# Two units of the samples' scores above one another in one tile, and zero rows below operands of few rows

## Chip, cores and metric

The kernel runs on one core of a Trainium2 chip. The metric is the time of one execution on the device in microseconds (us); the median of several executions is compared. TensorE multiplies matrices: its left operand has up to 128 rows (the partitions, over which it sums) and up to 128 columns, and it is loaded before the right operand streams through. VectorE, ScalarE and GpSimd do element work, and SyncE issues transfers; GpSimd also issues the gathers.

## What is computed

One inference step of a small decoder with two layers: a gated short convolution, then an attention over a shared latent (256 numbers a position) and a rotary key (32 numbers). One prompt of 1024 positions goes through it, and 8 samples with 4 new positions each, which attend to 2048 cached positions in 16 pages of 128. The part of a sample, cut to what the change touches:

```python
past_c  = cache_ckv[page_table].reshape(8, 2048, 256)      # gathered pages
past_kr = cache_krope[page_table].reshape(8, 2048, 32)
keys = concatenate([concatenate([past_c, c_new], 1), concatenate([past_kr, kr_new], 1)], -1)
q    = concatenate([einsum('blhd,chd->blhc', q_nope, w_uk), q_rope], -1)   # 16 heads
s    = einsum('bqhd,bkd->bhqk', q, keys) * SCALE            # 4 positions x 16 heads = 64 rows
p    = softmax(where(k_pos <= q_pos, s, neg))
o    = einsum('bhqk,bkc->bqhc', p, latent values)           # then w_uv, gate, w_out_mla
```

## The kernel before

The program runs in stages: the convolution layer (to about 500 us), the projections to latents and queries (to about 800), the prompt's attention (816 to 1085), a passage (to 1130), the samples' attention (to 1311), and the rest of the output projection (to 1370). A scheduler sets the order of instructions on every engine when the kernel is built, from the order of the code, the buffers of each pool, and its own simulation of time.

The samples' loop runs over 32 units: 8 samples of 4 units, each of 4 pages, 512 positions. All products are made of a high and a low part of their operands (`hi_of` on ScalarE, `lo_of` on VectorE or GpSimd), so three matmuls stand for one product. Step s of the loop

- issues a gather of latents, `cn`, five units ahead, on GpSimd's queue (`gather`, through `fetch`), and of rotary keys, `kn`, once a sample;
- turns the next unit's `cn` by eight 128x128 transposes on TensorE into `pc`, from which `ch` and `cl` are made (`take`);
- computes scores (`scores`): `ps` has 64 rows of products with the high part of the query and, below them, 64 with the low part; ScalarE copies the low half to `t`, and VectorE adds the halves into `st` and keeps the maximum in `tops`. After a sample's fourth unit `softmax` forms the maximum, the exponentials with their sums, and the reciprocal;
- turns the weights of the unit five steps back (`turn`): four transposes of `st`, 64 rows each, and for the fourth unit one of `own`, the weights of the 4 new positions; the result `pt` has a high and a low part;
- splits `cn` into `nh` and `nl` (`halve`), and weighs the unit six steps back (`weigh`): four pairs of products `po` with `nh` and `nl`, and behind the fourth unit two with `cvl` and `cvh`, the new positions' latents of all samples (32 rows);
- closes a sample seven steps back (`close`): sums the halves of `po` into `ot`, divides, and turns it by two transposes into `olt`.

Between these stand matmuls of the output projection (`left`, tile `pf`; 8 blocks of 24) as fill; they need `wmh` and `wml`, made from transfers `wor` on SyncE's queue. The last stage's products are `pr`. Buffers limit the run ahead: 9 of `cn`, 3 of `nh` and `nl`, 2 of `pt`, 2 of `st` (one a sample).

For the prompt, `divisors` writes the reciprocals of the softmax's sums, split in high and low parts, into four rows by SyncE's transfers, and `times` multiplies them on TensorE by `both`, a matrix of ones and zeros with four rows on partitions 64 to 67, so that 128 columns get their divisors. Seven pairs of heads do this with `rows` (the last four rows of `kr`) in the prompt's stage; the eighth uses `rr` in the passage.

Names in rows: `pc<-ident,cn` is a transpose by the identity matrix; `pp<-ident,st`, `pp<-ident,own` and `pp<-ident,ot` are the turns of weights, of own weights and of a finished sample; `pb<-rr,both` and `pm<-kr,both` are the divisors. In the profile's words PE is TensorE, PEld its loads of the left operand, DVE is VectorE, ACT ScalarE, POOL GpSimd, SP SyncE. Line L69 is the helper `mm`, L74 `hi_of`, L79 `lo_of`; the other lines are in the listing.

Of the kernel before, what the change touches and what calls it, by code (L numbers as in the profile page):

```python
# [21 lines left out]
P = 128  # L22
# [32 lines left out]
def decoder_step(ctx: ExitStack, tc: tile.TileContext, i, o):  # L55
# [611 lines left out]
    tops = new.tile([DN, NB, 5], F32, name="tops")  # L667
    both = new.tile([2 * DR + 4, P], F32R, name="both")[2 * DR:]
# [8 lines left out]
    krh, krl, rows = kr[:DR], kr[DR:2 * DR], kr[2 * DR:, :SEQ]  # L677
# [58 lines left out]
    dve.tensor_copy(both, both_)  # L736
# [173 lines left out]
    def new_scores():  # L910
# [7 lines left out]
        dve.tensor_reduce(tops[:, :, 4], fresh, AX.X, ALU.max)  # L918
# [163 lines left out]
    def divisors(lc, pl, rr_):  # L1082
# [7 lines left out]
        for x in range(2):  # L1090
            for n, src in enumerate((rh, rl)):
                sp.dma_start(f(rr_[2 * x + n:2 * x + n + 1]).rearrange("a (b c) -> a b c", c=8), f(src[:, x]))
# [214 lines left out]
    with ExitStack() as l8:  # L1307
# [33 lines left out]
        rr_ = sc.tile([2 * DR + 4, SEQ], F32R, tag="olt", name="rr")[2 * DR:]  # L1341
        divisors(pairs[NH // 2 - 1], new, rr_)

        sums = sc.tile([DN, NB, 4], F32, name="sums")
        own = sc.tile([DN, NB * (TS + LS)], F32, name="own")
        cv = sw.tile([TS, KV], F32, tag="ot", name="cv", bufs=1)
        cvh = sc.tile([TS, KV], F32R, name="cvh")
        cvl = sc.tile([TS, KV], F32R, name="cvl")

        sp.dma_start(cv, cnd)  # L1350
        hi_of(cvh, cv)
        lo_of(cvl, cv, cvh)
        pool.memset(own, 0.0)
# [61 lines left out]
        def scores(b, g):  # L1415
# [5 lines left out]
            t = sch.tile([DN, 512], F32, tag="t", name="t", bufs=2)  # L1421
            act.activation(t, ps[DN:], AF.Copy)
            if g == 0:
                state["s", b] = sw.tile([P, 4, 512], F32, tag="st", name="st")
            dve.tensor_tensor_reduce(state["s", b][:DN, g], ps[:DN], t, 1.0, NEG, ALU.add, ALU.max, tops[:, b, g:g + 1])

        def softmax(b):
            st = state["s", b]
            m = sw.tile([DN, 2], F32, tag="m", name="m")
            dve.tensor_reduce(m[:, 0:1], tops[:, b], AX.X, ALU.max)  # L1430
            dve.tensor_scalar(m[:, 1:2], m[:, 0:1], -SCALE, None, ALU.mult)
            mine = own[:, (TS + LS) * b:(TS + LS) * b + LS]
            act.activation(mine, fresh[:, b], AF.Exp, scale=SCALE, bias=m[:, 1:2], accum_out=sums[:, b, 0:1])
            for n in range(2):
                act.activation(st[:DN, 2 * n:2 * n + 2], st[:DN, 2 * n:2 * n + 2], AF.Exp, scale=SCALE, bias=m[:, 1:2], accum_out=sums[:, b, n + 1:n + 2])
# [290 lines left out]
```

## Time and profile before

| what | value |
|---|---|
| median of 3 executions | 1366.18 us (1363.27 to 1369.87) |
| the profiled execution | 1371.72 us, span of its trace 1369.9 us, mean granted clock of TensorE 0.971 |
| busy, share of the span | PE 95%, PEld 85%, DVE 63%, ACT 49%, POOL 44% |
| transfers | 131.87 MB, 96 GB/s in the mean |

All rows come from the one profiled execution. A row of a timeline gives the start, the duration, the engine, the line, the operation, result and operands, the shapes (64*128 is a left operand of 64 rows and 128 columns), and in brackets how long the engine had been idle before and what ended that. The starts of neighbouring matmuls are better to go by than their durations, which are modelled and overlap. A row of a window gives its bounds and length, the busy time of PE, PEld, DVE, ACT and POOL with the number of instructions, the granted clock of TensorE (1.00 is 2.4 GHz, 0.50 is 1.2), the busy share of the DMA engines, and GB/s. In the chain of waits every step is followed back from the last instruction to what released it.

### The profile page before, as it was taken

The page shows a single profiled execution, that of the slowest core. Times are in us where ns is not written, and L with a number is a line of the kernel's source. Part 1 is how long each engine was busy: PE and PEld are TensorE (multiplying, and loading weights), DVE is VectorE, ACT ScalarE, POOL GpSimd, SP SyncE. Part 2 cuts the span into 40 slices and gives each one's busy share as a digit, 9 for nine tenths or more (in the row PEclk, how much of TensorE's full clock was granted, in tenths as well). Part 3 has the DMA queues.
Part 4 walks back from the last instruction along what each step waited for, and adds up shares of the span by engine and source line. Part 5 has one row for each costly group of instructions (what it writes and reads, how often), then busy time and mean ns, then how long its engine had stood idle before and what let it go on. Part 6 is the DMA issues. An engine that isn't in the chain of part 4 may idle for free.

```text
span 1369.9 us, 22910 instructions
## 1 busy us (share of the span) xinstructions
PE 1295.0 (95%) x8142; PEld 1167.1 (85%) x8142; DVE 861.7 (63%) x1749; ACT 672.7 (49%) x1394; POOL 605.4 (44%) x828
## 2 busy tenths in 40 slices
PE   6899999999999999998899999999999878999997
PEld 6799999999978899998899878888888756777675
DVE  5776566666464445156623577877778668676865
ACT  5533333333243333222312377777767668777831
POOL 5465555555311133453320555555546634544421
PEclk8899999999999999999999999999999978999999
DMA  6122122122362232346730120121111276444454
GB/s 187 52 64 62 51 76 79 48 79 63 94 220 92 91 110 68 98 133 178 198 91 1 39 63 25 48 63 41 48 47 26 72 215 168 148 130 128 128 163 163
DMA packets 107022, 131.87 MB, mean 96 GB/s; under 512 B 21007, under 2 KB 80059, under 8 KB 106907
## 3 DMA queue, kind: packets, MB, share of 16 engines
q1 hardware_dynamic: 101659, 111.51, 27.6%
q0 software_dynamic: 5248, 18.88, 4.6%
q8 instruction: 65, 1.06, 0.3%
q14 instruction: 50, 0.41, 0.1%
HBM read 93.95 MB, written 28.78 MB: 90 GB/s over the span
## 4 chain that ended last, share of the span: by engine, by line
PE 72%; DMA 10%; DVE 8%; ACT 3%; issue 3%; POOL 2%; SPq 1%; DVEq 0%; POOLq 0%; ACTq 0%
PE pa L69 11%; PE b L69 10%; PE po L69 8%; PE c L69 7%; PE ps L69 7%; PE a L69 6%; PE pm L69 6%; PE pz L69 5%; PE pr L69 3%; DMA qh<-qdh 3%; PE pf L69 3%; DMA cn<-in_cache_ckv_dram,crow 2%; PE pk L69 2%; PE pt L69 1%; DVE mx L1044 1%
## 5 line engine op out<-in xcount | busy, mean ns | idle before, releaser
L79 DVE TENSOR_TENSOR wl<-raw,wh 128x512 fp32r<-128x512 f32 x86 | 71.3, 831 | 87.6 <-ACT wh L74 84.3
L74 ACT ACTIVATE wh<-raw 128x512 fp32r<-128x512 f32 x88 | 55.1, 630 | 129.7 <-PE pa L69 47.0
L1188 ACT ACTIVATE p<-ps 128x512 f32<-128x512 f32 (+1 forms) x192 | 93.2, 492 | 39.7 <-PE ps L69 32.1
L69 PE MATMUL pz<-ph,v 128*128 128x512 f32 (+3 forms) x384 | 104.5, 358 | 0.0
L74 ACT ACTIVATE ph<-p 128x512 fp32r<-128x512 f32 (+1 forms) x192 | 95.4, 526 | 17.8 <-POOL p L1193 16.8
L79 POOL TENSOR_TENSOR pl<-p,ph 128x512 fp32r<-128x512 f32 (+2 forms) x75 | 82.4, 1108 | 33.8 <-ACT ph L74 23.9
L79 DVE TENSOR_TENSOR pl<-p,ph 128x512 fp32r<-128x512 f32 (+3 forms) x117 | 81.0, 706 | 21.5 <-ACT ph L74 21.2
L79 POOL TENSOR_TENSOR nl<-cn,nh 128x256 fp32r<-128x256 f32 x64 | 59.8, 950 | 76.2 <-ACT nh L74 60.9
L1044 DVE TENSOR_REDUCE mx<-pm 128x1 f32<-128x16 f32 (+6 forms) x210 | 83.7, 423 | 9.9 <-PE pm L69 9.5
L1193 POOL TENSOR_SCALAR_AFFINE_SELECT p<-p 128x127 f32<-128x127 f32 (+1 forms) x128 | 47.4, 374 | 75.0 <-ACT p L1188 66.1
L69 PEld LDWEIGHTS pz<-ph,v 128*128 128x128 f32 x384 | 67.0, 193 | 6.4 <-ACT ph L74 0.3
L69 PE MATMUL ps<-qh,kh 97*128 97x512 f32 (+3 forms) x192 | 68.7, 358 | 1.9 <-DMA qh<-mr 0.9
L69 PE MATMUL pz<-pl,v 128*128 128x512 f32 (+1 forms) x192 | 69.0, 360 | 0.7 <-DVE pl L79 0.3
L69 PE MATMUL ps<-qh,kl 97*128 97x512 f32 (+3 forms) x192 | 66.9, 348 | 0.0
L69 PE MATMUL ps<-ql,kh 97*128 97x512 f32 (+3 forms) x192 | 66.8, 348 | 0.0
L69 PE MATMUL pa<-x1h,wh 128*128 128x352 f32 x288 | 64.3, 330 | 1.1 <-DVE big L861 1.1
L69 PE MATMUL pm<-kh,qh 128*128 128x144 f32 (+6 forms) x210 | 60.2, 340 | 5.4 <-DMA qh<-qdh 4.0
L74 ACT ACTIVATE wh<-s 128x512 fp32r<-128x512 f32 x48 | 30.0, 630 | 68.2 <-POOL s L174 27.2
L69 PE MATMUL pa<-x1h,wl 128*128 128x352 f32 x288 | 63.4, 326 | 0.0
L69 PE MATMUL pa<-x1l,wh 128*128 128x352 f32 x288 | 62.5, 325 | 0.0
L109 POOL TENSOR_SCALAR ta<-ss 128x1 f32<-128x1 f32 (+2 forms) x36 | 8.6, 240 | 118.9 <-ACT xa L624 51.1
L79 DVE TENSOR_TENSOR wl<-s,wh 128x512 fp32r<-128x512 f32 x45 | 44.3, 987 | 20.5 <-ACT wh L74 18.8
(483 smaller groups left out, 4426.6 us busy)
## 6 DMA issues: line engine op xcount, KB each, us to landing
raw<-in_w_in_conv_dram SPq DMA_DIRECT2D x32, 512.0 KB
raw<-in_w_in_mla_dram SPq DMA_DIRECT2D x12, 512.0 KB
qdh<-qxh SPq DMA_DIRECT2D x24, 256.0 KB
qdl<-qxl SPq DMA_DIRECT2D x24, 256.0 KB
qh<-qdh SPq DMA_DIRECT2D x16, 384.0 KB
ql<-qdl SPq DMA_DIRECT2D x16, 384.0 KB
raw<-in_w_out_conv_dram SPq DMA_DIRECT2D x8, 512.0 KB
x1d<-xa SPq DMA_DIRECT2D x8, 512.0 KB
```

The source lines that it names most:

```text
L69: return pe.matmul(out, a, b, start=start, stop=stop, **kw)
L74: return act.activation(out, src, AF.Copy, scale=scale)
L79: (eng or dve).tensor_tensor(out, src, f(hi), ALU.subtract)
L109: pool.tensor_scalar(t[:r], ss[:r], 1.0 / n, EPS, ALU.mult, ALU.add)
L1044: dve.tensor_reduce(mx[:, b, c:c + 1], pm[:, :off], AX.X, ALU.max)
L1188: act.activation(pt[:r, :n], ps[:r, :n], AF.Exp, scale=SCALE)
L1193: marks[h] = marks.get(h, []) + [pool.affine_select(pt[:r, :dn], pt[:r, :dn], [[1, dn]], ALU.is_ge, 0.0, base=META + c0 - t * P, channel_m ...
```

## The change

Two units share one tile of 128 partitions. The scores of an even unit go to partitions 0 to 63 and those of an odd unit to 64 to 127 of an `st` of 512 columns, of which there are five buffers instead of two of four times the width. `tops` and `sums` get 128 rows, and the maximum and the sums are joined over the two halves by small instructions of VectorE. The exponential runs twice over 128x512 instead of twice over 64x1024. `turn` transposes two units at once, by four 128x128 transposes, and `pt` holds both. The own positions get a turn of their own (`turn_own`), 128 columns of a `own` with 128 rows. Operands with few rows get zero rows up to 128 (`own`, `cvh`, `cvl`, `ot`), or 68 (`both`, `rows`, `rr`). The lags of the loop stay as they are. The weights `w_uv` come in four transfers into four tiles of `st`. The diff below leaves out context and the changed slices in the products of `w_uv`.

```diff
@@ -664,8 +664,8 @@
-    tops = new.tile([DN, NB, 5], F32, name="tops")
-    both = new.tile([2 * DR + 4, P], F32R, name="both")[2 * DR:]
+    tops = new.tile([P, NB, 3], F32, name="tops")
+    both = new.tile([2 * DR + 4, P], F32R, name="both")
@@ -674,7 +674,7 @@
-    krh, krl, rows = kr[:DR], kr[DR:2 * DR], kr[2 * DR:, :SEQ]
+    krh, krl, rows = kr[:DR], kr[DR:2 * DR], kr[:, :SEQ]
@@ -733,7 +733,8 @@
-    dve.tensor_copy(both, both_)
+    pool.memset(f(both[:2 * DR]), 0.0)
+    dve.tensor_copy(both[2 * DR:], both_)
@@ -915,7 +916,8 @@
-        dve.tensor_reduce(tops[:, :, 4], fresh, AX.X, ALU.max)
+        pool.memset(tops[DN:, :, 2], NEG)
+        dve.tensor_reduce(tops[:DN, :, 2], fresh, AX.X, ALU.max)
@@ -1089,7 +1091,7 @@
-                sp.dma_start(f(rr_[2 * x + n:2 * x + n + 1]).rearrange("a (b c) -> a b c", c=8), f(src[:, x]))
+                sp.dma_start(f(rr_[2 * DR + 2 * x + n:2 * DR + 2 * x + n + 1]).rearrange("a (b c) -> a b c", c=8), f(src[:, x]))
@@ -1338,19 +1340,23 @@
-        rr_ = sc.tile([2 * DR + 4, SEQ], F32R, tag="olt", name="rr")[2 * DR:]
+        rr_ = sc.tile([2 * DR + 4, SEQ], F32R, tag="olt", name="rr")
+        pool.memset(f(rr_[:2 * DR]), 0.0)
...
-        sums = sc.tile([DN, NB, 4], F32, name="sums")
-        own = sc.tile([DN, NB * (TS + LS)], F32, name="own")
-        cv = sw.tile([TS, KV], F32, tag="ot", name="cv", bufs=1)
-        cvh = sc.tile([TS, KV], F32R, name="cvh")
-        cvl = sc.tile([TS, KV], F32R, name="cvl")
...
-        sp.dma_start(cv, cnd)
-        hi_of(cvh, cv)
-        lo_of(cvl, cv, cvh)
-        pool.memset(own, 0.0)
+        sums = sc.tile([P, NB, 4], F32, name="sums")
...
+        own = sc.tile([P, TS * (NB - 1) + P], F32, name="own")
+        cvh = sc.tile([P, KV], F32R, name="cvh")
+        cvl = sc.tile([P, KV], F32R, name="cvl")
+        ot = sc.tile([P, KV], F32, name="ot")
...
+        for t in (ot, sums, own, f(cvh), f(cvl)):
+            pool.memset(t, 0.0)
+        sp.dma_start(ot[:TS], cnd)
+        hi_of(cvh[:TS], ot[:TS])
+        lo_of(cvl[:TS], ot[:TS], cvh[:TS])
@@ -1418,42 +1424,51 @@
-            t = sch.tile([DN, 512], F32, tag="t", name="t", bufs=2)
-            act.activation(t, ps[DN:], AF.Copy)
-            if g == 0:
-                state["s", b] = sw.tile([P, 4, 512], F32, tag="st", name="st")
-            dve.tensor_tensor_reduce(state["s", b][:DN, g], ps[:DN], t, 1.0, NEG, ALU.add, ALU.max, tops[:, b, g:g + 1])
+            mine, other = (slice(0, DN), slice(DN, P))[::1 - 2 * (g % 2)]
+            t = sch.tile([P, 512], F32, tag="t", name="t", bufs=2)
+            act.activation(t[mine], ps[other], AF.Copy)
+            if g % 2 == 0:
+                state["s", b, g // 2] = sw.tile([P, 512], F32, tag="st", name="st", bufs=5)
+            dve.tensor_tensor_reduce(state["s", b, g // 2][mine], ps[mine], t[mine], 1.0, NEG, ALU.add, ALU.max, tops[mine, b, g // 2:g // 2 + 1])
...
-            st = state["s", b]
-            m = sw.tile([DN, 2], F32, tag="m", name="m")
+            m = sw.tile([P, 3], F32, tag="m", name="m")
...
-            dve.tensor_scalar(m[:, 1:2], m[:, 0:1], -SCALE, None, ALU.mult)
-            mine = own[:, (TS + LS) * b:(TS + LS) * b + LS]
-            act.activation(mine, fresh[:, b], AF.Exp, scale=SCALE, bias=m[:, 1:2], accum_out=sums[:, b, 0:1])
+            dve.tensor_copy(m[:DN, 1:2], m[DN:, 0:1])
+            for rr in (slice(0, DN), slice(DN, P)):
+                dve.tensor_scalar(m[rr, 2:3], m[:DN, 0:1], m[:DN, 1:2], -SCALE, ALU.max, ALU.mult)
...
-                act.activation(st[:DN, 2 * n:2 * n + 2], st[:DN, 2 * n:2 * n + 2], AF.Exp, scale=SCALE, bias=m[:, 1:2], accum_out=sums[:, b, n + 1:n + 2])
-            dve.tensor_reduce(sums[:, b, 3:4], sums[:, b, :3], AX.X, ALU.add)
-            dve.reciprocal(sums[:, b, 3:4], sums[:, b, 3:4])
...
-        def turn(b, g):
...
-            st = state["s", b]
-            if b == NB - 1:
-                pp = pss.tile([P, 512], F32, tag="s", name="pp")[:, :5 * DN].rearrange("p (n c) -> p n c", c=DN)
-            else:
-                pp = psp.tile([P, 5, DN], F32, tag="p", name="pp")
-            for n in range(4):
-                pe.transpose(pp[:, n], st[:DN, g, n * P:(n + 1) * P], ident[:DN, :DN])
-            pt = sw.tile([P, 5, P], F32R, tag="pt", name="pt", bufs=PTB)
-            if g == 3:
-                pe.transpose(pp[:TS, 4], own[:, TS * b:TS * b + TS], ident[:DN, :DN])
-                hi_of(pt[:TS, 4, :DN], pp[:TS, 4])
-            hi_of(pt[:, :4, :DN], pp[:, :4])
-            if g == 3:
-                lo_of(pt[:TS, 4, DN:], pp[:TS, 4], pt[:TS, 4, :DN])
-            lo_of(pt[:, :4, DN:], pp[:, :4], pt[:, :4, :DN])
-            state["q", b, g] = pt
+                st = state["s", b, n]
+                act.activation(st, st, AF.Exp, scale=SCALE, bias=m[:, 2:3], accum_out=sums[:, b, n + 1:n + 2])
+            mine = own[:DN, (TS + LS) * b:(TS + LS) * b + LS]
+            act.activation(mine, fresh[:, b], AF.Exp, scale=SCALE, bias=m[:DN, 2:3], accum_out=sums[:DN, b, 0:1])
...
+        def turn(b, n):
...
+            st = state.pop(("s", b, n))
...
+            pp = (pss.tile([P, 4, 2, DN], F32, tag="s", name="pp") if b == NB - 1 else psp.tile([P, 4, 2, DN], F32, tag="p", name="pp"))
+            for k in range(4):
+                pe.transpose(pp[:, k].rearrange("p e c -> p (e c)"), st[:, k * P:(k + 1) * P], ident)
+            pt = sw.tile([P, 4, 2, P], F32R, tag="pt", name="pt", bufs=PTB)
+            hi_of(pt[:, :, :, :DN], pp)
+            lo_of(pt[:, :, :, DN:], pp, pt[:, :, :, :DN])
+            state["q", b, n] = pt
...
+        def turn_own(b):
...
+            pp = psp.tile([P, 4, 2, DN], F32, tag="p", name="pp")
+            pe.transpose(pp[:, 0].rearrange("p e c -> p (e c)"), own[:, TS * b:TS * b + P], ident)
+            pt = sw.tile([P, P], F32R, tag="po", name="pto", bufs=3)
+            hi_of(pt[:, :DN], pp[:, 0, 0])
+            lo_of(pt[:, DN:], pp[:, 0, 0], pt[:, :DN])
+            state["q", b, "own"] = pt
...
+            s = sums[:, b]
+            dve.tensor_reduce(s[:, 3:4], s[:, :3], AX.X, ALU.add)
+            dve.tensor_copy(s[:DN, 0:1], s[DN:, 3:4])
+            dve.tensor_tensor(s[:DN, 3:4], s[:DN, 3:4], s[:DN, 0:1], ALU.add)
+            dve.reciprocal(s[:DN, 3:4], s[:DN, 3:4])
@@ -1467,7 +1482,7 @@
-            pt = state.pop(("q", b, g))
+            pt = state["q", b, g // 2][:, :, g % 2]
@@ -1477,19 +1492,20 @@
-                mm(po[:DN], pt[:TS, 4, :DN], cvl, False, False)
-                mm(po, pt[:TS, 4], cvh, False, True)
+                pt = state.pop(("q", b, "own"))
+                mm(po[:DN], pt[:, :DN], cvl, False, False)
+                mm(po, pt, cvh, False, True)
...
-            t = sw.tile([DN, KV], F32, tag="ot", name="ot", bufs=1)
+            t = ot[:DN]
...
-            dve.tensor_scalar(t, t, sums[:, b, 3:4], None, ALU.mult)
-            pp = psp.tile([P, 5, DN], F32, tag="p", name="pp")
+            dve.tensor_scalar(t, t, sums[:DN, b, 3:4], None, ALU.mult)
+            pp = psp.tile([P, 4, 2, DN], F32, tag="p", name="pp")
...
-                pe.transpose(pp[:, c], t[:, c * P:(c + 1) * P], ident[:DN, :DN])
-            act.activation(olt[:, :, :, LS * b:LS * b + LS], pp[:, :2].rearrange("p c (h t) -> p c h t", t=LS), AF.Copy)
+                pe.transpose(pp[:, c].rearrange("p e c -> p (e c)"), ot[:, c * P:(c + 1) * P], ident)
+            act.activation(olt[:, :, :, LS * b:LS * b + LS], pp[:, :2, 0].rearrange("p c (h t) -> p c h t", t=LS), AF.Copy)
@@ -1560,7 +1576,13 @@
-            for lag, what in ((LAGT, turn), (LAGH, halve), (LAGW, weigh)):
+            if 0 <= s_ - LAGT < len(units):
+                b, g = units[s_ - LAGT]
+                if g % 2 == 0:
+                    turn(b, g // 2)
+                elif g == 1:
+                    turn_own(b)
+            for lag, what in ((LAGH, halve), (LAGW, weigh)):
```

Order on GpSimd in the passage, before: `kn` and `cn` are gathers, and the fill of `own` stands between them.

```order
L1339 DMA cn<-in_cache_ckv_dram,crow 128x1024
L1339 DMA kn<-in_cache_krope_dram,krow 128x512
L1353 MEMSET own 64x288
L1339 DMA cn<-in_cache_ckv_dram,crow 128x1024 x6
L1339 DMA kn<-in_cache_krope_dram,krow 128x512
```

And after:

```order
L1341 DMA kn<-in_cache_krope_dram,krow 128x512
L1344 MEMSET rr 64x1024
L1356 MEMSET ot 128x256
L1356 MEMSET sums 128x32
L1356 MEMSET own 128x352
L1356 MEMSET cvh 128x256
L1356 MEMSET cvl 128x256
L1341 DMA cn<-in_cache_ckv_dram,crow 128x1024 x6
```

Six fills now stand ahead of the six gathers, where one stood.

Order on ScalarE in the passage, before: `ch` is a turned unit's high part, `wmh` that of the output weights, `kh` that of the rotary keys.

```order
L74 ACTIVATE cvh<-cv 32x256
L1422 ACTIVATE t<-ps 64x512
L74 ACTIVATE kh<-kx 128x512
L74 ACTIVATE ch<-pc 128x512 x3
L74 ACTIVATE wmh_12807<-wor 128x512
L74 ACTIVATE ch<-pc 128x512
L74 ACTIVATE wmh_12808<-wor 128x512
```

And after:

```order
L74 ACTIVATE cvh<-ot 32x256
L74 ACTIVATE wmh_12814<-wor 128x512
L74 ACTIVATE wmh_12815<-wor 128x512
L74 ACTIVATE ch<-pc 128x512 x4
L74 ACTIVATE wmh_12816<-wor 128x512
```

Two conversions of output weights stand ahead of the four `ch` instead of between them.

Order on TensorE around one turn in the middle of the loop, before:

```order
L69 MATMUL pf<-wmh_12814,gl 128x512
L1447 MATMUL pp<-ident,st 128x64 x4
L1450 MATMUL pp<-ident,own 32x64
L69 MATMUL po<-nh,pt 128x256
L69 MATMUL po<-nl,pt 64x256
```

And after:

```order
L69 MATMUL pf<-wmh_12820,gl 128x512
L1452 MATMUL pp<-ident,st 128x128 x4
L1413 MATMUL pc<-ident,cn 128x128 x4
L69 MATMUL po<-nh,pt 128x256
L69 MATMUL ps<-cl,qs 64x512 x2
L69 MATMUL po<-nl,pt 64x256
```

The four transposes of a turn have 128 columns of result for two units, the own positions' turn stands elsewhere, and products of other steps are mixed in between.

## Rows read from the trace of the kernel before

**Rows 1.** Page, part 4: the chain that ended last, by engine.

```profile
PE 72%; DMA 10%; DVE 8%; ACT 3%; issue 3%; POOL 2%; SPq 1%; DVEq 0%; POOLq 0%; ACTq 0%
```

**Rows 2.** Windows: span, length, busy us by engine (x), PEclk, DMA share, GB/s.

```profile
816.00:1085.00 269.00, 262.41 (x1480) 227.76 (x1479) 206.42 (x637) 190.50 (x441) 151.30 (x250) 0.99 0.16 42
...
1130.00:1311.00 181.00, 166.41 (x963) 129.38 (x962) 137.62 (x286) 142.59 (x291) 86.81 (x97) 0.96 0.47 143
```

**Rows 3.** Chain of waits through the samples' loop, 1130 to 1311, by line.

```profile
by line: PE pf L69 21.5%; PE po L69 13.0%; DMA cn<-in_cache_ckv_dram,crow 9.7%; PE ps L69 8.6%; PE pc L1407 6.8%; issue 6.7%; DVE nl L79 4.3%; PE pp L1447 3.8%; DMA wor<-in_w_out_mla_dram 2.7%; POOL nl L79 2.7%; ACT nh L74 2.2%; DMA kp<-kh 
```

**Rows 4.** TensorE timeline in the loop: start, us, line, out<-in, rows*columns, xcount.

```profile
1183.05 1.03 PE L1407 MATMUL pc<-ident,cn 128*128 128x128 f32 x8
...
1184.15 0.62 PE L69 MATMUL ps<-cl,qs 128*64 128x512 f32 x2
...
1184.85 0.40 PE L69 MATMUL ps<-ch,qs 128*128 128x512 f32 x1
1185.18 0.46 PE L1447 MATMUL pp<-ident,st 64*128 64x64 f32 x4
...
1185.79 0.28 PE L69 MATMUL po<-nl,pt 128*64 128x256 f32 x1
...
1186.49 0.28 PE L69 MATMUL po<-nl,pt 128*64 128x256 f32 x1
...
1187.41 0.62 PE L69 MATMUL ps<-cl,qs 128*64 128x512 f32 x2
```

**Rows 5.** TensorE timeline at one divisors' pair of the prompt.

```profile
911.74 0.27 PE L1052 MATMUL pm<-ident,m 128*8 128x128 f32 x1
911.95 0.73 PE L69 MATMUL pm<-kr,both 4*128 4x512 f32 x2
912.60 0.42 PE L69 MATMUL pm<-cth,up 128*128 128x348 f32 x1
912.86 0.32 PE L69 MATMUL pm<-ctl,up 128*128 128x348 f32 x1
```

**Rows 6.** Windows at either clock (columns as Rows 2; PEclk third from the end).

```profile
1117.00:1120.40 3.40, 3.40 (x16) 2.96 (x15) 2.04 (x4) 1.98 (x4) 0.91 (x1) 0.50 1.09 349
1123.80:1127.20 3.40, 2.31 (x13) 1.38 (x13) 1.71 (x6) 2.32 (x5) 0.00 (x0) 1.00 0.81 244
1127.20:1134.00 6.80, 6.50 (x26) 4.92 (x26) 5.21 (x11) 5.39 (x12) 0.03 (x1) 0.50 0.35 94
1161.40:1164.80 3.40, 3.40 (x13) 2.81 (x12) 3.10 (x6) 3.40 (x7) 0.70 (x2) 0.50 0.66 163
1236.50:1239.90 3.40, 3.36 (x16) 3.36 (x17) 2.71 (x6) 2.66 (x4) 0.00 (x0) 0.50 0.69 208
1301.30:1304.70 3.40, 3.38 (x17) 3.05 (x17) 2.01 (x4) 1.84 (x4) 0.74 (x2) 0.50 0.90 330
```

**Rows 7.** Passage: timelines of GpSimd, TensorE, ScalarE, then a group by form.

```profile
1108.35 0.35 POOL L1353 MEMSET own<- 64x288 f32 x1
...
1116.13 1.97 PE L1407 MATMUL pc<-ident,cn 128*128 128x128 f32 x8 [4.41 <-DMA cn<-in_cache_ckv_dram,crow]
...
1125.35 0.47 PE L69 MATMUL pb<-rr,both 4*128 4x512 f32 x1 [0.70 <-DMA rr<-rl]
...
1120.11 0.62 ACT L74 ACTIVATE wmh<-wor 128x512 fp32r<-128x512 f32 x1
...
L984 POOL MEMSET qh<- 32x1024 f32 x1 | 0.9, 942 | 0.0
```

**Rows 8.** Groups by form, 1085 to 1320 us: xcount, busy, mean ns, idle.

```profile
L1425 DVE CUSTOM_DVE_ANT_0 st<-ps,t 64x512 f32<-64x512 f32 x32 | 21.4, 674 | 9.1 <-PE pp L1447 7.5 <-ACT t L1422 1.1 <-issue 0.5
...
L1435 ACT ACTIVATE st<-st,m 64x1024 f32<-64x1024 f32 x16 | 18.2, 1140 | 0.0
...
L1447 PE MATMUL pp<-ident,st 64*128 64x64 f32 x128 | 15.0, 241 | 4.2 <-DVE pt L79 3.3 <-ACT olt L1492 0.5 <-ACT st L1435 0.4
```

**Rows 9.** TensorE timeline at the last sample's close.

```profile
1311.24 0.31 PE L1491 MATMUL pp<-ident,ot 64*128 64x64 f32 x2 [1.39 <-DVE ot L1488]
```

More of the change, by code (lines that the diff above doesn't have):

```diff
@@ L1570, in decoder_step @@
                 done += 1
-        uv = sw.tile([P, 4, 512], F32, tag="st", name="uv").rearrange("p (c a) m -> p c (a m)", c=2)
-        sp.dma_start(uv, i["w_uv"].rearrange("(c p) h d -> p c (h d)", p=P))
+        uv = [[sw.tile([P, 512], F32, tag="st", name="uv", bufs=5) for _ in range(2)] for _ in range(2)]
+        for c in range(2):
+            for n in range(2):
+                sp.dma_start(uv[c][n], i["w_uv"].rearrange("(c p) h d -> p c (h d)", p=P)[:, c, 512 * n:512 * n + 512])
         po = pss.tile([P, 8, 2 * TS], F32, tag="s", name="pu")
@@ L1575, in decoder_step @@
             for c in range(2):
-                mm(po[:, pr], uv[:, c, pr * P:(pr + 1) * P], olt[:, c, 2 * pr:2 * pr + 2].rearrange("p h t -> p (h t)"), c == 0, c == 1)
+                mm(po[:, pr], uv[c][pr // 4][:, pr % 4 * P:(pr % 4 + 1) * P], olt[:, c, 2 * pr:2 * pr + 2].rearrange("p h t -> p (h t)"), c == 0, c == 1)
         for e in range(2):
```

## The prediction, made before the changed kernel ran

> **What bounds the kernel now.** I read the page first: the chain of work that ended last is 72% TensorE and 10% transfers [rows 1]. So work on TensorE is worth something, but not everywhere at the same rate, and the stages come next. In the prompt's attention (816 to 1085 us) TensorE is busy 262.4 of 269 us; in the samples' loop (1130 to 1311) 166.4 of 181 us [rows 2]. Both stages hold instructions that the change touches. The chain of the loop alone tells at what rate a saved microsecond of TensorE comes back there: its pf, po, ps, pc and pp add up to 53.7%, and the rest is transfers of cn and wor, nl on two engines, nh and issue [rows 3]. So about 0.55 of a microsecond for each one saved on TensorE, and nearly all of it in the prompt's stage. How expensive short operands are is read from starts of neighbouring instructions on TensorE, since its ends are modelled [rows 4, 5]. Last I read where the granted clock is at half [rows 6] and the passage between the stages, where the change adds work to GpSimd [rows 7].
>
> **Transposes of scores, part by part.** Full-height work runs at a steady pace: the three score products from 1184.15 to 1184.85 take 0.70 us, 0.233 each, and the six value products from 1185.79 to 1186.49 take 0.70, 0.117 each. Eight 128-row transposes and one score product lie between 1183.05 and 1184.15: 1.10 less 0.233 leaves 0.109 a transpose. The four 64-row transposes stand between a score product at 1184.85 and the second value product at 1185.79: 0.94 less 0.233 and 0.117 leaves 0.59, or 0.148 each, though they do half the columns [rows 4]. There are 128 of them, 16 a sample [rows 8]. They become 8 a sample of 128 rows: 4 x 0.59 = 2.36 us become 8 x 0.109 = 0.87, so 1.49 saved. The two transposes of a finished sample go from 0.148 to 0.109 each, 0.08 saved. The turn of the sample's own four columns stays one instruction; I count nothing for it.
>
> **Own products.** From 1186.49 to the second score product at 1187.41 four starts take 0.92 us: a value product, cvl and cvh on 32 rows, a score product [rows 4]. At full height they would take 3 x 0.117 + 0.233 = 0.58, so 0.34 saved. A sample thus gives 1.49 + 0.08 + 0.34 = 1.91 us, eight give 15.3 us of TensorE. At 0.55 that is **-8.4 us**. Its bounds: nothing, if the loop then waits for something else, and the whole -15.3.
>
> **Prompt's divisors.** Two products of `both` with 4 rows follow a transpose of m: from 911.74 to 912.86 the four starts take 1.12 us [rows 5]. At the pace of full rows they would take 2 x 0.233, a 348/512 part of 0.233, and 0.109: 0.73. The 0.39 saved comes 7 times before the loop, 2.7 us; the stage is 97.5% TensorE, so **-2.6 us**. If 68 rows still change the mode of the array as 4 do, it is nothing.
>
> **Clock.** In the passage TensorE took up work at 1116.13 with eight 128-row transposes, was busy all of 1117.0 to 1120.4 at half clock (0.50, the lower of its two levels), and by 1123.8 the clock was full [rows 6, 7]. From 1123.8 TensorE was busy 2.31 of 3.40 us with full transposes, the two 4-row products and four 64-row turns; then the clock fell to 0.50 for 6.8 us. Three more stretches of 3.4 us at half follow (1161.4, 1236.5, 1301.3). Half of the work done in the four, 6.50 + 3.40 + 3.36 + 3.38, is 8.3 us: that is the most that the clock can give. Only the first follows directly on the operations that become taller. Its 6.50 busy us are worth at most 3.25; I take **-2.5 us**, nearest to it, with 0 and -8.3 as bounds.
> The Trainium skill, page "TensorE: Matmul & The Clock Gate", Part 4 (PE-mode transpose), says that the full clock "doesn't engage" for transposes, which are not counted as busy in the same way. By that rule the term would be 0; the stretch from 1116.13, which begins with eight transposes and behind which the clock rose, speaks against it.
>
> **Added: fills with zero.** On GpSimd's queue one fill (own, 0.35 us) stood ahead of six gathers; now six do. Priced by columns from the rows of 1024 (0.94) and 288 (0.35): rr 0.94, three of 256 at 0.32, own of 352 at 0.40, sums 0.14: 2.4 us, so 2.1 more [rows 7]. Queued behind them are the gathers of cn, and TensorE waited 4.41 us for such a gather at 1116.13, so nothing hides them: **+2.1 us**. Below, it is 0, if the transfers and not their issue set that landing. Above, the two conversions of wmh, now ahead of four ch on ScalarE, add 2 x 0.62 [rows 7] if they wait for their transfer: +3.4. SyncE's read of the own rows into ot now waits for the fill of ot, and the wor and the divisors' transfers are queued behind it; the pb product at 1125.35 had waited 0.70 for them, which the same +3.4 covers. The earlier fills (zero rows of both, and of tops) lie some 300 us before the stage in which they are used, and I cost them at nothing.
>
> **ScalarE, VectorE, buffers.** Two exponentials of 64x1024 at 1.14 us become two of 128x512. By columns that halves them, 1.1 us a sample (an estimate from that row) [rows 8]. VectorE's score additions waited 7.5 us in sum for the turns of an earlier sample, for the buffer of st [rows 8]; five smaller tiles end that. VectorE gets three small instructions a sample more. ScalarE and VectorE together hold under a tenth of the loop's chain, so I count these at 0, with 4 us either way. One turn now converts 512 columns at once, but the order leaves a step of the loop between a turn and its use.
>
> **The end.** Before, 24 products pr of the last stage stood among the last samples' work, after it 10: 14 x 0.233 = 3.3 us move behind the loop, if the places where they stood are idle now. TensorE idled 1.39 us there at 1311.24 [rows 9]; after the change four pr fill that very wait. I take half, **+1.6 us**, bounds 0 and 3.3.
>
> **The sum.** -8.4 - 2.6 - 2.5 + 2.1 + 1.6 = -9.8 us. Against the profiled execution (1371.7, its span 1369.9 and 1.8 around it) that is 1361.9 us; that execution lies 5.5 us over the median of the three runs, so for the median, 1366.2, I forecast **1356.4 us**.
>
> **The rivals.**
> *All of it shows (B).* The loop is 92% TensorE; if every microsecond comes back, and all four half-clock stretches go: -15.3 - 2.7 - 8.3 + 2.1 = -24.2, 1342.0 us. For it: the share of busy time. Against it: the chain, in which over 40% isn't TensorE.
> *Saved work becomes waiting (C).* Gathers set the loop's pace: cn holds 9.7% of its chain, and nl and nh, which gate the next gathers, another 9% [rows 3]. Then the loop gives nothing and its clock neither: -2.6 + 2.1 + 1.6 = +1.1, 1367.3 us. Against it: in GpSimd's order some ten of the later 22 gathers stand one nl earlier and three later.
> *The waiting costs the clock (D), the slower side.* As C, but the 1.9 us a sample, now idle, let the clock fall more often, as it fell behind 1123.8 where TensorE had been busy 2.31 of 3.40 us. One more stretch like that of 1301.3 costs half of its 3.38 us, 1.7. Four more, one in every second sample, make +1.1 + 6.8 = +7.9, 1374.1 us. It decides from the fourth on: three leave it within half a percent.
> *Height is worth nothing (L): the change does not do what it says.* Only the halved number of score turns helps: 8 x 0.109 a sample, 7.0 in eight, at 0.55 -3.8; with +2.1 + 1.6 that is -0.1, 1366.1 us. Against it: 0.148 beside 0.109 for a transpose [rows 4].
> The Trainium skill, same page, section "LDWEIGHTS (loading the stationary operand)", says just that: a load of 32x128 takes as long as one of 128x128, since the columns decide. The rows of the trace disagree as far as starts go: 0.92 us where full height makes 0.58.
> *The clock does not move (E).* The sum without its term: -7.3, 1358.9 us.
>
> **How the numbers follow.** Forecast 0.45, C 0.20, B 0.11, D 0.11, L 0.07, E 0.06. The range 1342 to 1371 leaves out D and about half of B, under 2 in 10. About 0.5%, 6.8 us, is what a measurement of this kernel can tell from no change. Faster by more: 0.36 of the forecast's 0.45 (its own bounds reach past 1359.4), B, and 0.04 of E: 0.51. Within: C, L and the rest of E and of the forecast: 0.37. Slower: D and 0.01 of others: 0.12.
>
> **What would show it.** The turns: four 128-row pp transposes within 0.45 us of starts, and cvl and cvh at 0.117 each; if they keep 0.59 and 0.2, L holds. Divisors: 0.73 instead of 1.12 us at each `both` pair, and the samples' first score some 2.6 us earlier but for the fills. Fills: TensorE's wait of 4.41 us at the first gathered page grows to about 6.5. Clock: no half-speed stretch behind the first turns. In the loop, TensorE's busy time falls by about 15 us and its idle time grows by under 7; if it grows by all of 15, C or D is right, told apart by the half-clock stretches. The prediction is wrong if the passage, in which the order of ScalarE, SyncE and GpSimd changes, loses more than 3.4 us, or if the last samples run out of fill and the end takes more than 3.3.

## The result and the profile after

The changed kernel takes 1377.37 us in the median of 11 executions (1372.93 to 1379.77), the kernel before 1369.61 us in 11. The ratio is 1.0055, with a 95% interval of 1.0036 to 1.0074: some 7.5 us slower. The forecast was 1356.4 us with a range up to 1371, so the prediction was wrong in sign and in size. Of the distance of 21 us, 3.4 us lie in the kernel before, whose median of three was 1366.18 us when the forecast was made.

In the page of the changed kernel, the chain that ended last answers to [rows 1]:

```profile
PE 70%; DMA 11%; DVE 9%; ACT 3%; issue 2%; POOL 2%; SPq 1%; DVEq 0%; POOLq 0%; ACTq 0%
```

TensorE's share fell from 72 to 70%, transfers and VectorE gained one point each. That says little; the stages say more. I cut both traces at the same instructions on TensorE: the second product of the seventh prompt pair (`both`), the first `pb` of the passage, the last `po` of the samples, the end. Windows of the kernel before (columns as in [rows 2]), for passage, loop and end:

```profile
1078.70:1125.40 46.70, 34.94 (x169) 26.53 (x167) 30.58 (x64) 28.01 (x59) 21.85 (x34) 0.85 0.61 179
1125.40:1309.60 184.20, 170.26 (x977) 131.57 (x977) 139.53 (x289) 144.90 (x295) 86.04 (x95) 0.95 0.47 143
1309.60:1369.90 60.30, 51.57 (x236) 40.23 (x235) 35.30 (x50) 15.25 (x32) 8.47 (x19) 0.94 0.47 157
```

The same three of the changed kernel:

```profile
1074.60:1123.10 48.50, 34.95 (x170) 26.17 (x169) 31.22 (x64) 29.07 (x58) 23.51 (x40) 0.86 0.62 183
1123.10:1298.20 175.10, 155.25 (x896) 126.02 (x894) 142.12 (x300) 131.20 (x274) 85.46 (x95) 0.96 0.44 130
1298.20:1375.70 77.50, 64.27 (x255) 48.67 (x253) 39.62 (x56) 19.09 (x38) 9.36 (x19) 0.86 0.47 162
```

The passage got 1.8 us longer, the loop 9.1 us shorter, the end 17.2 us longer. In the loop TensorE is busy 155.3 instead of 170.3 us and idle 19.9 instead of 13.9 (18 `pr` of 0.233 us, 4.2 in all, have left it, as shown below). At the end the granted clock is 0.86 in the mean instead of 0.94. So what the change was about is there, and the loss is in a place that it does not mention: the last products of the output projection.

Why they are late is seen on ScalarE. Eight conversions `wmh` of the output weights' second half must be done before all `pr` can run. In the kernel before, the first and the last of the eight:

```profile
1281.83 1.14 ACT L74 ACTIVATE wmh<-wor 128x512 fp32r<-128x512 f32 x2
...
1302.67 0.63 ACT L74 ACTIVATE wmh<-wor 128x512 fp32r<-128x512 f32 x1 [2.95 <-DMA wor<-in_w_out_mla_dram]
```

The last `po` there starts at 1309.6 us, so all eight are finished 6 us ahead of it. The changed kernel's timeline of ScalarE has the eight here (the first row holds two):

```profile
1293.01 1.14 ACT L74 ACTIVATE wmh<-wor 128x512 fp32r<-128x512 f32 x2
...
1297.90 0.63 ACT L74 ACTIVATE wmh<-wor 128x512 fp32r<-128x512 f32 x1 [2.72 <-DMA wor<-in_w_out_mla_dram]
...
1300.74 0.62 ACT L74 ACTIVATE wmh<-wor 128x512 fp32r<-128x512 f32 x1
...
1305.80 0.63 ACT L74 ACTIVATE wmh<-wor 128x512 fp32r<-128x512 f32 x1 [3.19 <-DMA wor<-in_w_out_mla_dram]
1309.05 0.63 ACT L74 ACTIVATE wmh<-wor 128x512 fp32r<-128x512 f32 x1 [2.62 <-DMA wor<-in_w_out_mla_dram]
1309.93 0.63 ACT L74 ACTIVATE wmh<-wor 128x512 fp32r<-128x512 f32 x1 [0.25 <-DMA wor<-in_w_out_mla_dram]
1317.01 0.63 ACT L74 ACTIVATE wmh<-wor 128x512 fp32r<-128x512 f32 x1 [6.45 <-DMA wor<-in_w_out_mla_dram]
```

Its last `po` starts at 1298.2 us: two of the eight are converted 4 us before it, and the last one starts 19 us behind it. TensorE's timeline at the end shows who pays:

```profile
1301.41 0.49 PE L69 MATMUL pr<-wmh,gh 128*128 128x512 f32 x1 [0.89 <-ACT wmh L74]
1302.66 7.09 PE L69 MATMUL pu<-olt,uv 128*128 128x64 f32 x32 [0.76 <-ACT olt L1508]
1309.51 0.78 PE L69 MATMUL pr<-wml,gh 128*128 128x512 f32 x1
...
1313.23 0.50 PE L69 MATMUL pr<-wml,gh 128*128 128x512 f32 x1 [0.81 <-DVE wml L79]
...
1317.69 0.79 PE L69 MATMUL pr<-wmh,gh 128*128 128x512 f32 x1 [3.03 <-ACT wmh L74]
...
1320.36 0.79 PE L69 MATMUL pr<-wmh,gh 128*128 128x512 f32 x1 [0.72 <-ACT gh L74]
```

The 32 matmuls with `w_uv` (`pu`) take 7.1 us at half clock, and `pr` waits 0.89, 0.81 and 3.03 us for `wmh` and `wml`. The granted clock of two stretches there (columns as above, PEclk is the third figure from the end):

```profile
1302.50:1312.60 10.10, 9.76 (x38) 8.65 (x38) 4.98 (x9) 1.99 (x4) 0.00 (x0) 0.50 0.74 267
1316.20:1326.20 10.00, 7.79 (x17) 5.38 (x18) 4.02 (x5) 2.26 (x4) 1.23 (x2) 0.50 0.19 59
```

It is at 0.50, the lower of its two levels, for most of 1302 to 1326 us. Before the first fall TensorE was busy 2.38 of 4.30 us (1298.2 to 1302.5), before the second 1.43 of 3.60 us (1312.6 to 1316.2).

The built order shows the same before any time is measured. On ScalarE, before, where the conversions begin (`nh` is a high part of the gathered latents for the last samples):

```order
L1486 ACTIVATE ot<-po 64x256
L1422 ACTIVATE t<-ps 64x512
L74 ACTIVATE wmh_15286<-wor 128x512
L74 ACTIVATE wmh_15287<-wor 128x512
L1433 ACTIVATE own,sums<-fresh,m 64x4
```

And after:

```order
L74 ACTIVATE nh<-cn 128x512 x3
L1508 ACTIVATE olt<-pp 128x32x4
L74 ACTIVATE wmh_15219<-wor 128x512
L74 ACTIVATE wmh_15220<-wor 128x512
L74 ACTIVATE nh<-cn 128x512 x2
L74 ACTIVATE wmh_15221<-wor 128x512
```

Before, 13 conversions `nh` stand behind the first two `wmh`; after, 2. The products follow: 24 `pr` stood ahead of the last `po`, now 6 do (both traces; the prediction had counted 24 and 10 in the order). On SyncE the four transfers of `w_uv` (`uv`) stand ahead of the third `wor`, where one `uv` stood behind the seventh:

```profile
1263.47 18.22 SPq L1596 DMA_DIRECT2D uv<-in_w_uv_dram  x4
...
1295.16 1.47 SPq L1524 DMA_DIRECT2D wor<-in_w_out_mla_dram  x2
...
1313.20 0.33 SPq L1524 DMA_DIRECT2D wor<-in_w_out_mla_dram  x1
```

The four take 18 us to be issued, since each needs a buffer of `st`. The last two go out at 1280.87 and 1281.36 us, just behind two turns (`pp` of `st`) that end at 1280.80 and 1281.24, of which the second belongs to the last sample. They are out by 1281.7, 13 us before the third `wor`: that one waits for the first pair of conversions, `wmh` and `wml`, and `wmh` starts at 1293.01. So it is the place in ScalarE's order that makes the weights late here, and not the wait for a buffer as such.

The theory, A: the end is late because the weights are converted late, and they stand late in the built order because `uv` lacks a buffer. Its rival, B: the end is slow because the loop is shorter and its fill and transfers no longer suffice.

### The profile page after: what moved, and what is told of

Same layout as the page of the kernel before. It is cut to its first block, busy times and chain, and to the rows that moved or that the text cites. A ratio compares the mean times of both kernels' runs of the same rounds, so it can differ in the third digit from the quotient of the medians.

```text
span 1375.7 us, 22771 instructions
## 1 busy us (share of the span) xinstructions
PE 1290.2 (94%) x8078; PEld 1169.4 (85%) x8078; DVE 867.2 (63%) x1765; ACT 663.8 (48%) x1378; POOL 608.7 (44%) x835
## 4 chain that ended last, share of the span: by engine, by line
PE 70%; DMA 11%; DVE 9%; ACT 3%; issue 2%; POOL 2%; SPq 1%; DVEq 0%; POOLq 0%; ACTq 0%
PE b L69 10%; PE pa L69 10%; PE po L69 8%; PE c L69 7%; PE ps L69 6%; PE a L69 6%; PE pm L69 5%; PE pz L69 5%; PE pr L69 3%; DMA qh<-qdh 3%; PE pf L69 3%; DMA cn<-in_cache_ckv_dram,crow 2%; PE pk L69 1%; PE pt L69 1%; PE pc L1413 1%
## 5 line engine op out<-in xcount | busy, mean ns | idle before, releaser
L79 POOL TENSOR_TENSOR nl<-cn,nh 128x256 fp32r<-128x256 f32 x64 | 56.4, 896 | 74.3 <-ACT nh L74 40.3
L1195 POOL TENSOR_SCALAR_AFFINE_SELECT p<-p 128x127 f32<-128x127 f32 (+1 forms) x128 | 47.5, 375 | 72.4 <-ACT p L1190 65.3
L69 PE MATMUL pm<-kh,qh 128*128 128x144 f32 (+6 forms) x210 | 60.3, 339 | 5.2 <-DMA qh<-qdh 4.6
L79 DVE TENSOR_TENSOR wl<-s,wh 128x512 fp32r<-128x512 f32 x45 | 44.3, 987 | 20.0 <-ACT wh L74 18.8
```

The lines of the kernel that those rows point to most:

```text
L69: return pe.matmul(out, a, b, start=start, stop=stop, **kw)
L79: (eng or dve).tensor_tensor(out, src, f(hi), ALU.subtract)
L1195: marks[h] = marks.get(h, []) + [pool.affine_select(pt[:r, :dn], pt[:r, :dn], [[1, dn]], ALU.is_ge, 0.0, base=META + c0 - t * P, channel_m ...
```

## The experiments

Times of a kernel are compared by the ratio to the kernel before on the same chips. A table of all traces stands behind the runs.

**e1_six_st**: one buffer more.

```diff
-                state["s", b, g // 2] = sw.tile([P, 512], F32, tag="st", name="st", bufs=5)
+                state["s", b, g // 2] = sw.tile([P, 512], F32, tag="st", name="st", bufs=6)
-        uv = [[sw.tile([P, 512], F32, tag="st", name="uv", bufs=5) for _ in range(2)] for _ in range(2)]
+        uv = [[sw.tile([P, 512], F32, tag="st", name="uv", bufs=6) for _ in range(2)] for _ in range(2)]
```

> The changed kernel with six buffers of st instead of five; nothing else differs in the code. In the built order the conversions of the second half's output weights (wmh, wml for pr) then stand on ScalarE with 13 conversions nh of the loop still behind the first of them, as in the kernel before; with five buffers only 2 are behind. Theory A (the weights of the second half are converted too late; the loop itself gained its 11 us): the loop still ends about 11 us earlier than before, no pr product waits for wmh or wml by more than 0.5 us, and the time is 1356 to 1361 us. Rival B (the end is slow because the fill of the loop runs out or transfers are contended, whatever the order of the weights): the time stays at 1374 to 1378 us.

Measured: 1364.53 us, ratio 0.9969 (0.9951 to 0.9986). Against the changed kernel's 1.0055 that is 0.86% or 11.8 us less, by one buffer. The time is 3.5 us above the range that A gave. A took the 11 us by which the loop ended earlier for the change's gain; 1.8 us of them lie ahead of the first pair of divisors already (its second product starts at 828.3 instead of 830.1), and the 4.2 us of the 18 `pr` had only moved out of the loop. Here the last `po` starts 6.3 us earlier than before (1303.3). Another part of the expectation missed too: `pr` waits twice for `wmh`, 1.2 us in sum and up to 0.9, where at most 0.5 was expected. Windows of loop and end:

```profile
1125.10:1303.30 178.20, 159.25 (x914) 128.83 (x912) 147.64 (x306) 134.85 (x279) 84.15 (x95) 0.96 0.49 145
1303.30:1363.80 60.50, 51.76 (x237) 40.20 (x235) 35.38 (x50) 15.43 (x32) 9.88 (x19) 0.95 0.46 157
```

The end takes 60.5 us, as before (60.3), with the clock at 0.95. B falls: the loop has the changed kernel's shorter work, and its end is as quick as before. On TensorE the two kernels run the same order through the first 158 us of the loop and differ only behind that, so the buffer acts at the end alone.

**e7_one_uv**: five buffers, but the last tile of `uv` is its own.

```diff
-        uv = [[sw.tile([P, 512], F32, tag="st", name="uv", bufs=5) for _ in range(2)] for _ in range(2)]
+        uv = [[sw.tile([P, 512], F32, tag="uv", name="uv", bufs=1) if (c, n) == (1, 1) else sw.tile([P, 512], F32, tag="st", name="uv", bufs=5) for n in range(2)] for c in range(2)]
```

> The changed kernel with five buffers of st as it is, and the last of the four w_uv transfers into a tile of its own. The order of the second half's conversions is then that of e1 (13 nh left behind the first). If the place of the weights is the cause, the time is that of e1 within 2 us (1362 to 1367). If a sixth buffer for the scores was what helped in e1, it stays near 1377 us.

Measured: 1363.55 us, ratio 0.9972 (0.9954 to 0.9991), that of e1. It isn't the scores that lacked a buffer; `uv` did.

**e2_late_weights**: the reverse, in the kernel before.

```diff
-            act.activation(olt[:, :, :, LS * b:LS * b + LS], ...
+            state["c", b] = act.activation(olt[:, :, :, LS * b:LS * b + LS], ...
-        w1 = columns(w7, 1)
+        with tc.issue_after(state["c", 6].ins):
+            w1 = columns(w7, 1)
```

> The kernel before, with only this: the conversions of the second half's output weights are queued on ScalarE behind the close of sample 6, which gives the same row in its order as in the changed kernel (2, 2 and then 0 conversions nh left behind). Theory A: the loop ends as before (last po near 1309.6 us of the trace) and the end is 12 to 18 us later: 1381 to 1388 us. Rival B: within 3 us of the kernel before, 1367 to 1373 us.

Measured: 1375.89 us (4 runs), ratio 1.0065 (1.0041 to 1.0089), 8.9 us slower. Loop and end in its trace:

```profile
1119.20:1299.30 180.10, 164.79 (x960) 125.37 (x959) 132.44 (x285) 142.17 (x291) 87.38 (x95) 0.97 0.45 133
1299.30:1369.20 69.90, 60.16 (x254) 46.41 (x253) 39.75 (x56) 18.76 (x37) 8.64 (x19) 0.90 0.52 177
```

The end is 9.6 us longer than before, the loop 4.1 us shorter, as it lacks 18 `pr`. On TensorE its order is that of the kernel before for the first 164 us of the loop. That the late place of the second half's weights alone (their transfers and both conversions are queued later together) makes the old kernel slower is shown; the time lies between the two expectations, above B's 1373 and below A's 1381, and A's loop that ends as before didn't come. The traced execution, 1370.91 us, is the fastest of the four, and that of the kernel before, 1371.72, lies 2.1 us above its median, so the 8.9 us come from the times, and the traces only show the stage. The last `wmh` starts 13.7 us behind the last `po` here (1313.0 and 1299.3), 18.8 us in the changed kernel, and the extra idle time and clock at the end cost 5 us here, 13 there (sums below the table). Why the last transfers are 5 us later still in the changed kernel wasn't tried apart.

**e4_divisors**: the kernel before with only the 68-row operands `both`, `rows` and `rr` and their fills (the diff's first hunks).

> The kernel before, with only the divisors' operands of 68 rows (both, rows, rr, with their fills). As forecast: 0.39 us less at each of seven pairs, 2.6 us, less up to 0.9 us for the fill of rr ahead of the gathers: 1.7 to 2.6 us under the kernel before. If 68 rows cost what 4 do: 0 to 0.9 us above it.

Measured: 1364.53 us, ratio 0.9975 (0.9960 to 0.9991): 3.4 us faster, with the forecast's 1.7 to 2.6 inside the interval.

**e3_short_own**: e1 with short operands for the own positions and the close (the conversions behind the turn of `own`, not shown here, are shortened alike).

```diff
-            pe.transpose(pp[:, 0].rearrange("p e c -> p (e c)"), own[:, TS * b:TS * b + P], ident)
+            pe.transpose(pp[:TS, 0, 0], own[:DN, TS * b:TS * b + TS], ident[:DN, :DN])
...
-                mm(po[:DN], pt[:, :DN], cvl, False, False)
-                mm(po, pt, cvh, False, True)
+                mm(po[:DN], pt[:TS, :DN], cvl[:TS], False, False)
+                mm(po, pt[:TS], cvh[:TS], False, True)
...
-                pe.transpose(pp[:, c].rearrange("p e c -> p (e c)"), ot[:, c * P:(c + 1) * P], ident)
+                pe.transpose(pp[:, c, 0], ot[:DN, c * P:(c + 1) * P], ident[:DN, :DN])
```

> Run e1 with the zero rows taken out of use in the own positions' turn and products and in the close: own is turned from 64 rows, cvl and cvh multiply 32 rows, ot is turned from 64 rows (the fills with zero stay). If height counts as the starts in the trace say, TensorE spends 0.34 + 0.08 us more a sample, 3.4 us in eight, and at 0.55 the time is 1.9 us above that of e1 (1 to 3.4). If height is worth nothing it is within 0.7 us of e1.

Measured: 1365.53 us, ratio 0.9979 (0.9965 to 0.9994), 1.4 us above e1 by the ratios, and the intervals overlap. By time alone this is unclear. In the traces TensorE's work in the loop is 3.3 us larger (table: the mean of e3 and e5 against the four kernels at full height), against 3.4 forecast.

**e5_lean**: e3 with only `own` and `sums` filled and the eighth pair of divisors in 4 rows.

```diff
-        for t in (ot, sums, own, f(cvh), f(cvl)):
+        for t in (sums, own):
             pool.memset(t, 0.0)
...
-        pool.memset(f(rr_[:2 * DR]), 0.0)
...
-        mm(pb, both, rr_[:, hs], True, True)
+        short = slice(2 * DR, None) if pr == NH // 2 - 1 else slice(None)
+        mm(pb, both[short], rr_[short, hs], True, True)
```

> Run e3 (six st, short own and close) without the fills that it does not need: only own and sums are filled, the eighth divisors' pair has 4 rows again and rr is not filled; so 0.55 us of fills ahead of the six gathers instead of 2.4. If the fills are what makes the passage longer (from the seventh prompt pair to the eighth: 46.7 us in the kernel before, 44.8 with the same code in e2, 48.5 in the changed kernel, 50.7 in e1, 49.0 in e3), it shrinks by about 2 us and the time is 1.5 to 2.5 us below e3. If the passage is longer for the new order of ScalarE and SyncE, the time stays within 0.7 us of e3.

Measured: 1366.59 us, ratio 0.9987 (0.9972 to 1.0002), 1.1 us above e3 instead of 2 below; the intervals overlap, so the two times aren't told apart, but the 1.5 to 2.5 us did not show. Its passage and loop:

```profile
1076.20:1122.30 46.10, 34.74 (x168) 26.28 (x167) 31.16 (x63) 27.66 (x56) 22.01 (x36) 0.85 0.61 175
1122.30:1306.40 184.10, 165.64 (x913) 129.35 (x913) 150.14 (x306) 137.17 (x281) 86.96 (x95) 0.95 0.48 145
```

The passage did shrink, from 49.0 to 46.1 us. The loop is 184.1 us instead of 178.9 in e3. Of these 5.2 us the table puts 3.1 on the half clock and 1.0 each on work and idle time. So without the fills the passage is shorter, but the expectation took the rest of the kernel for unchanged, and it is not: TensorE's order differs from e3's through the whole loop. Whether that order costs the time isn't shown, since the half clock, the largest part, changes from one execution to the next.

**e6_fill_vector**: e1 with the six fills on VectorE (`dve.memset` for `pool.memset`).

> Run e1 with the same six fills made by VectorE instead of GpSimd, so that no fill stands ahead of the gathers. If GpSimd's queue is what they cost, 2 us below e1; if VectorE, which makes cl there, is needed as much, within 1 us of e1 or above.

Measured: 1365.12 us, ratio 0.9990 (0.9975 to 1.0005), 2.9 us above e1, with intervals that just overlap. TensorE's timeline in its passage:

```profile
1109.48 0.77 PE L69 MATMUL ps<-ch,qs 128*128 128x512 f32 x1 [2.64 <-DVE tops L1432]
...
1112.63 1.97 PE L1413 MATMUL pc<-ident,cn 128*128 128x128 f32 x8 [1.96 <-DMA cn<-in_cache_ckv_dram,crow]
```

The wait for the gather is 1.96 us, but a new one of 2.64 us for VectorE's score additions stands ahead of it. The passage takes 50.6 us, against 50.7 in e1. The fills are no cheaper there; they hold up another engine's queue.

The stages of all traces, in us. Work is the sum over TensorE's products in the loop of the time from their start to the next start (or to their own end, if that is earlier), halved where the granted clock was 0.50; the other half is "lost to half clock"; idle is what remains. A product's own end is modelled and lies later than the next product can start, so a short wait behind it counts as work. The column "without pr, pb" leaves these out of the work, since their number in the loop differs.

| kernel | passage | loop | work without pr, pb | lost to half clock | idle | end |
|---|---|---|---|---|---|---|
| before | 46.7 | 184.2 | 154.4 | 8.5 | 14.0 | 60.3 |
| e2 late weights | 44.8 | 180.1 | 157.5 | 4.9 | 15.5 | 69.9 |
| e4 divisors | 45.1 | 187.2 | 156.2 | 7.7 | 15.7 | 58.1 |
| e3 short own | 49.0 | 178.9 | 149.2 | 5.0 | 17.4 | 60.4 |
| e5 lean | 46.1 | 184.1 | 149.9 | 8.1 | 18.4 | 59.7 |
| changed | 48.5 | 175.1 | 146.9 | 5.9 | 19.6 | 77.5 |
| e1 six st | 50.7 | 178.2 | 145.3 | 6.6 | 18.7 | 60.5 |
| e7 one uv | 47.5 | 175.6 | 146.4 | 1.7 | 20.4 | 60.4 |
| e6 fills on VectorE | 50.6 | 179.9 | 146.3 | 5.0 | 21.2 | 58.3 |

By the same sums the end, up to the last `pr`, has 49.4 us of work, 1.5 lost to half clock and 1.7 idle before; 54.7, 8.9 and 6.9 in the changed kernel; 49.4, 1.7 and 1.9 in e1; 54.5, 5.1 and 3.4 in e2. So of the 17.2 us at the end 5.3 are moved products, 7.4 are clock and 5.2 are waits (less 0.7 behind the last `pr`). Each row is one execution; work repeats within 1 to 2 us, the clock does not.

## Why the prediction was wrong, step by step

**The end is the step that failed.** The prediction saw 14 products `pr` move behind the loop and priced the move at 0 to 3.3 us, as if the products were free to run at once. It didn't ask why they moved. The same order had the answer, on ScalarE (2 `nh` instead of 13 behind the weights) and on SyncE (four `uv` ahead of the `wor`), and the prediction looked at these engines only in the passage. Measured: 11.8 us between e1 and the changed kernel. The prediction's last sentence did name an end of more than 3.3 us as a sign of being wrong, but no rival and no price stood for it. Without this the kernel would have been 4.2 us faster (e1), not 7.5 us slower. The description of the change had the cause in one line: five small buffers in place of two large ones, and `uv` in four of them.

**The turns of scores were priced rightly, but the loop gave back less than the rate of 0.55.** I took one group at 1185.18 [rows 4] with the time that it takes to enter and leave it, 0.59 us for four. A full-height group in e1:

```profile
1197.40 0.28 PE L69 MATMUL po<-nl,pt 128*64 128x256 f32 x1
1197.53 0.60 PE L1452 MATMUL pp<-ident,st 128*128 128x128 f32 x4
1197.88 0.36 PE L69 MATMUL po<-nh,pt 128*128 128x256 f32 x1
1198.08 0.28 PE L69 MATMUL po<-nl,pt 128*64 128x256 f32 x1
```

From 1197.40 to 1198.08 it is 0.68 us; less 0.117 for each of the two value products, four transposes cost 0.44, where the forecast had 4 x 0.109. Over the groups at full clock with no wait beside them, four transposes of 64 rows cost 0.56 us in the mean of 14 before (median 0.59), and four of 128 rows 0.44 in the mean of 11 in e1. For 32 and 16 groups that makes 18.0 and 7.1 us: 11.0 saved (an estimate from these means, for all groups), where the forecast had 11.9.

By the table (e3 and e5 against before, e2 and e4) the pairs save only 6.5 us of work in the loop (156.0 less 149.5). Of the 4.5 us between, 1.9 stand in products ahead of an idle gap, which count up to their modelled end (22 and 24 such gaps in e3 and e5, 9 to 15 in the three others), and 1.1 in value products behind one another; the rest wasn't separated.

The table's own sum doesn't depend on that division. Against 156.0 us of work and 15.0 idle (the mean of before, e2 and e4) the four full-height kernels have 146.2 and 20.0, so 9.8 - 5.0 = 4.8 us came back, where the forecast had 8.4. Of the 9.8 us that is 0.49; of the 14.3 that the starts give (11.0 and the 3.3 below) it is 0.34. So the mis-sized term is the loop's rate, as far as the starts tell. TensorE's wait for the gather `cn` in the loop grew from 5.8, 5.9 and 8.2 us (before, e2, e4) to 8.7, 10.1, 8.9 and 9.7 (changed, e1, e7, e6), 2.7 of the 5.0. So rival C was half true, as the chain had said.

**The own products and the close were right.** In the changed kernel:

```profile
1298.06 0.28 PE L69 MATMUL po<-cvl,pto 128*64 128x256 f32 x1
1298.18 0.28 PE L69 MATMUL po<-cvh,pto 128*128 128x256 f32 x1
```

`cvl` starts 0.12 us before `cvh`, the pace of full rows, as forecast. By the table (149.5 less 146.2) all of it is 3.3 us, where the forecast had 3.4.

**The prompt's divisors were right.** In the changed kernel:

```profile
910.17 0.27 PE L1054 MATMUL pm<-ident,m 128*8 128x128 f32 x1
910.20 0.71 PE L69 MATMUL pm<-kr,both 68*128 68x512 f32 x2
910.74 0.33 PE L69 MATMUL pm<-cth,up 128*128 128x348 f32 x1
910.91 0.32 PE L69 MATMUL pm<-ctl,up 128*128 128x348 f32 x1
```

From the transpose of m to the second product with `up` it is 0.74 us, where 0.73 was forecast and [rows 5] had 1.12; the six other pairs have 0.69 to 0.74. The 2.6 us lie inside the interval of e4 (1.2 to 5.5 us). Rival L, that height is worth nothing, falls here, for the own products and for the price of the turns, though the table's 6.5 us are near its 7.0.
The Trainium skill, page "TensorE: Matmul & The Clock Gate", section "LDWEIGHTS (loading the stationary operand)", lets the columns of a load decide and not its rows. The loads of these traces agree: `both` takes 183 ns with 4 rows before and 191 with 68 after, `cvh` 184 with 32 rows before and 187 with 128 in e1, all of 128 columns. So the rows that the prediction held against the page don't speak against it: what height changes here is the time between the starts of the products, and not that of a load.

**The clock came out about as forecast, by a mean.** 7.0 us were lost to the half clock in the loops of before, e2 and e4, 4.8 in the four full-height ones; -2.2 us against -2.5. But single executions lie between 1.7 and 8.5, so this is not shown to be the change's doing. D, the rival on the slower side, named a falling clock, and the time that it gave, 1374.1, is near the measured one. That is a coincidence: in the loop the clock did not get worse, at the end it did, for a reason that D doesn't have.

**The fills were under-sized.** GpSimd's fills after the change, and the first gather behind them:

```profile
1104.00 0.97 POOL L1344 MEMSET rr<- 64x1024 f32 x1
1104.89 0.33 POOL L1356 MEMSET ot<- 128x256 f32 x1
1105.14 0.14 POOL L1356 MEMSET sums<- 128x32 f32 x1
1105.20 0.41 POOL L1356 MEMSET own<- 128x352 f32 x1
1105.54 0.33 POOL L1356 MEMSET cvh<- 128x256 f32 x1
1105.79 0.33 POOL L1356 MEMSET cvl<- 128x256 f32 x1
1106.28 0.95 POOL L1341 DMA_INDIRECT cn<-in_cache_ckv_dram,crow  x1 [0.16 <-issue]
```

They take 2.3 us up to the gather, near the 2.4 worked out from columns. TensorE's wait for it:

```profile
1112.35 1.97 PE L1413 MATMUL pc<-ident,cn 128*128 128x128 f32 x8 [5.17 <-DMA cn<-in_cache_ckv_dram,crow]
```

It grew from 4.41 [rows 7] to 5.17 us, by less than the 2.1. But the passage as a whole is 48.9 us in the mean of the four kernels with GpSimd's fills, and 45.5 in before, e2 and e4 (which fills `rr` alone): +3.4, at the upper bound, though single executions of the same code differ by 1.9 (before and e2) to 3.2 us (e1 and e7). e5 took 1.9 us of fills away and the passage 2.9 us; which other instruction of the passage carries the rest wasn't separated.

**The sum again with the measured sizes:** -2.7 for the divisors, -9.8 + 5.0 - 2.2 = -7.0 for the loop, +3.4 for the passage make -6.3 us, inside e1's interval (-6.7 to -1.9) but 2.1 below its -4.2, which stays open. With the +11.8 of the end it is +5.5, inside the changed kernel's interval (+4.9 to +10.1); as the 11.8 is the distance of these two kernels, that is no second proof. How the scheduler comes from the missing buffer to the late place of the conversions wasn't seen: that the buffer is the cause is shown by e1 and e7, that the late place of the weights costs time by e2. Both e1 and e7 beat the two kernels, by 0.3% against the one before.

## What to carry to other kernels

When the order shows instructions that move, ask for every one of them what it waits for, and look at that engine's order too; instructions that move for no reason of their own are the sign that something they need has moved. A tile that gets smaller buffers changes what else fits into them: whatever borrows the same buffers later (here the weights of the last stage) has to be followed to the end of the program. And a price that is read from starts can be right while less comes back: the share of an engine in the chain of waits, 0.55 here, was no more than a guess at the rate, and 4.8 us came back of the 8.4 that it promised.

## What the runs showed of the hardware that was not expected

Four transposes of 64-row operands among other products cost 0.59 us in the median of 14 groups in the kernel before; four of 128 rows, whose moving operand is twice as wide, cost 0.44 in that of 11 in e1. Most of the difference lies at the border: the product ahead of a 64-row group is followed 0.09 us later than at its pace, that ahead of a 128-row group at its pace. Operands of 32 rows cost more than full ones: from its start to the next, `cvh` takes 208 ns and `cvl` 169 in the median of 8 before, 119 and 116 in e1, while their loads take 184 and 128 ns before, 187 and 134 in e1. And half clock was dearer than waiting: at the end of the changed kernel 5.2 us of extra idle time came with 7.4 us lost to half clock, as two stretches of some 10 us at 0.50 followed stretches in which TensorE was busy 2.38 of 4.30 and 1.43 of 3.60 us.
